# The next tile's preparation in a recurrent chain, issued behind the first half of the present tile's step

## The chip, the cores and the metric

The kernel runs on one core of a Trainium2 chip. Its time is the device time of one execution in microseconds (us). Engines are named as in the profile: PE (matrix multiplies; PEld its weight loads), DVE (the vector engine), ACT (the scalar engine), POOL (GpSimd) and SP (which issues the DMAs here). Each engine works through its own list of instructions in order; semaphores tell one engine that another, or a DMA, is done.

## The reference, cut to what matters

The model is two layers deep. In each layer 2304 tokens (256 of context, 2048 latent) are projected and pass three parallel groups of heads: a state-space scan, a gated delta rule (GDN) in both directions, and softmax attention. The part that the change touches is the GDN's scan over chunks of 64 tokens, for each of 4 heads and each direction:

```python
def step(S, inp):
    qd, kd, u_i, w_i, a_i, d_i = inp
    v_new = u_i - jnp.einsum('bhcd,bhde->bhce', w_i, S)
    o = jnp.einsum('bhcd,bhde->bhce', qd, S) + jnp.einsum('bhij,bhje->bhie', a_i, v_new)
    S = S * d_i[..., None, None] + jnp.einsum('bhcd,bhce->bhde', kd, v_new)
    return S, o
```

Every chunk needs the state S of the chunk before, so the 36 chunks of a layer are a chain. Attention needs nothing of it.

## The kernel before, in words

All values are 32-bit. In each layer the input projection comes first, then gating, the preparation of the GDN's chunk matrices (written to device memory), the state-space scan, then attention, and at the end the output projection. Attention is a list of 24 units of one head and 512 queries (`attention`, lines 623 to 675). For each unit, matmuls `pq` give scores of which DVE takes row maxima (`mx`, L533); then matmuls `pst` (L562, L563) give scores again, ACT takes the exponential (`pe`, L565), ACT and DVE split it into a high and a low part (`ph`, L570; `pl`, L571), and matmuls `po` (L556) multiply with the values. Three PSUM banks serve `pq` and `pst` while the chain runs.

`gdn_chain` (lines 1006 to 1182) runs beside attention, in the stretches of about 1340 to 1700 us (first layer) and 3300 to 3700 us (second). It handles both directions at once, one tile of 128 tokens of each direction per step, 18 steps to a layer, each of two halves (`for s in range(2)`), since a chunk is half a tile. Three functions make a step's work:

- `load(u)` (L1036) issues a tile's DMAs from SP into buffers that rotate among three tiles: `acv` (chunk matrices), `xu` and `xt` (parts of the triangular inverse), `kq` (keys and queries, called `kqc` in the profile) and `er` (decays). A buffer can be filled again only after the step three tiles earlier has read it.
- `prep(u)` (L1058) makes the loaded tile ready: DVE multiplies the keys by the decays (`kq[:, 0]`, L1060) and, where an output is wanted, masks `acv[:, :, 0]` (L1065), both in place; POOL makes `kdw` (L1062) and multiplies the queries (L1064); PE makes 16 small matmuls `pv` (L1071), ACT copies them to `vt` (L1075), PE makes 16 more from `vt` (L1080), and ACT copies these into `xu` (called `xf` in the profile; L1083).
- `step(u)` (L1086) does the two halves. In each, PE multiplies the state with the keys (L1104), DVE subtracts (`r`, L1108), PE multiplies by the inverse (L1118) and the queries (L1113), ACT copies `V` (L1123), PE makes the update and the output (L1127, L1129), and DVE adds the update to the decayed state `sd` (POOL, L1106), which gives the next state (`Sn`, called `Sc` in the profile; L1131).

`out(u)` (L1141) finishes an output tile. The loop at L1174 calls, for each u, `load(u + 2)`, `prep(u + 1)`, `step(u)` and `out` of a tile before. The order in which the calls are written isn't the order on the engines: the framework's scheduler places each instruction by a simulation of its own, and prefers what was written earlier among what it holds ready. Within `step` some matmuls are pinned by `behind` (L1002), which tells the scheduler that one instruction must stand after another of the same engine, with no semaphore.

Of the kernel before, what the change touches and what calls it, by code (L numbers as in the profile page):

```python
# [12 lines left out]
ALU = mybir.AluOpType  # L13
# [4 lines left out]
P = 128  # L18
# [66 lines left out]
def hybrid_kernel(ctx, tc, x, c, ctx_in, c_ctx, norm_w, w_mod, b_mod, w_in, conv_w, conv_b, ssd_A_log,  # L85
                  ssd_dt_bias, ssd_D, ssd_norm_w, gdn_A_log, gdn_dt_bias, gdn_norm_w, q_norm_w, k_norm_w,
                  w_out, cst_in, rope_in, eye_in, out):
    nc = tc.nc
# [23 lines left out]
    with tc.tile_pool(reuse_waits="tile", name="ini", bufs=1) as ini:  # L112
# [6 lines left out]
                                in1=sch[:, :, 0:2].bitcast(F32).rearrange("p k j -> p j k"), op=ALU.subtract)  # L119
# [124 lines left out]
    for l in range(DEPTH):  # L244
# [20 lines left out]
        with ExitStack() as ax:  # L265
# [118 lines left out]
            for g, (t0, ntl) in enumerate(GRP):  # L384
                for bi, (kind, c0, w, arg) in enumerate(blocks):
# [3 lines left out]
                    if kind == "n":  # L389
                        for u in range(ntl):  # L390
# [12 lines left out]
                            if arg < 2:  # L403
# [6 lines left out]
                                else:  # L410
# [7 lines left out]
                                    for o0, s0, n0 in ((0, 0, 50), (50, 62, 256)):  # L418
                                        nc.scalar.activation(out=zn[:, o0:o0 + n0], in_=ps[:, s0:s0 + n0], func=AF.Tanh, scale=0.5)
                                        nc.vector.scalar_tensor_tensor(out=zn[:, o0:o0 + n0], in0=zn[:, o0:o0 + n0], scalar=1.0,  # L420
                                                                       in1=ps[:, s0:s0 + n0], op0=ALU.add, op1=ALU.mult)
# [10 lines left out]
                    else:  # L432
                        for m in range(w // P):
# [12 lines left out]
                            for sb, (s0, sn) in enumerate(((0, 256), (256, 512)) if g == 0 else ((0, 384), (384, 384))):  # L446
# [6 lines left out]
                                for k in range(KD):  # L453
                                    for ww, hh in ((wh, hi), (wh, lo), (wl, hi)):
                                        nc.tensor.matmul(ps, ww[:, k, m * P:(m + 1) * P], hh[:, k, s0:s0 + sn],  # L455
                                                         start=(n == 0), stop=(n == 3 * KD - 1))
# [11 lines left out]
                            if kind == "t":  # L468
# [7 lines left out]
                                                               in1=acc[:, :n0], op0=ALU.mult, op1=ALU.add)  # L476
# [9 lines left out]
                                else:  # L486
                                    b0 = t0 * P - 1
# [3 lines left out]
        with ExitStack() as bx:  # L491
# [510 lines left out]
            def behind(mm, prev):  # L1002
                tc.add_manual_dep(mm.ins, prev.ins.name, mybir.DependencyInfo(
                    mybir.DependencyClass.NoSync, mybir.DependencyReason.DATA), reason="order")

            def gdn_chain(rq):
# [6 lines left out]
                with ExitStack() as gx:  # L1013
# [41 lines left out]
                            nc.sync.dma_start(er[dk[d]], eg_d[d:d + 1, :, u].to_broadcast([64, 4, P]))  # L1055
                        return u, xu, xt, kq, er, acv

                    def prep(u, xu, xt, kq, er, acv):  # L1058
                        want_o = u >= ot0
                        nc.vector.tensor_tensor(out=kq[:, 0], in0=kq[:, 0], in1=er, op=ALU.mult)  # L1060
                        kdw = gw.tile([P, 2, 4, 64], F32, name="kdw")
                        nc.gpsimd.tensor_tensor(out=kdw, in0=acv[:, :, 3], in1=kdc[:, u, :, :, None].to_broadcast([P, 2, 4, 64]), op=ALU.mult)  # L1062
                        if want_o:
                            nc.gpsimd.tensor_tensor(out=kq[:, 1], in0=kq[:, 1], in1=er, op=ALU.mult)  # L1064
                            nc.vector.tensor_tensor(out=acv[:, :, 0], in0=acv[:, :, 0], in1=msk[:, None, None, :].to_broadcast([P, 2, 4, 64]), op=ALU.mult)  # L1065
                        pv = slot("pv")
                        pvv = pv[:, 0:256].rearrange("p (c h n) -> p c h n", c=2, h=4)
                        for c in range(2):
                            for h in range(4):
                                for d in range(2):  # L1070
                                    nc.tensor.matmul(pvv[b1[d], c, h, :], acv[b0[d], 1 - c if d else c, 1, h, c1[d]], xt[b0[d], c, h, :],  # L1071
                                                     start=True, stop=True, tile_position=(b0[d].start, b1[d].start))
                        vt = gw.tile([P, 2, 4, 32], F32, name="vt")
                        for d in range(2):
                            nc.scalar.activation(out=vt[b1[d]], in_=pvv[b1[d]], func=AF.Copy, scale=-1.0)  # L1075
                        pzv = pv[:, 256:512].rearrange("p (c h n) -> p c h n", c=2, h=4)
                        for c in range(2):
                            for h in range(4):
                                for d in range(2):
                                    nc.tensor.matmul(pzv[b0[d], c, h, :], vt[b1[d], c, h, :], xu[b1[d], c, h, c1[d]],  # L1080
                                                     start=True, stop=True, tile_position=(b1[d].start, b0[d].start))
                        for d in range(2):
                            nc.scalar.copy(out=xu[b0[d], :, :, c1[d]], in_=pzv[b0[d]])  # L1083
                        return xu, kq, acv, kdw

                    def step(u, S, xu, kq, acv, kdw):  # L1086
                        tl = (u, rev(u))
                        want_o = u >= ot0
                        second = (u >= 1) if u < TC else (u >= TC + (NT - TC) // 2)
                        ox = op_ = None  # L1090
                        if want_o:
                            ox = gw.tile([P, 2, 4, 64], F32, name="ox")
                            if second:
                                op_ = gw.tile([P, 2, 256], F32, name="op_", bufs=1)
                                for d in range(2):
                                    by_chunk(d, o_d[tl[d]], op_)
                        for s in range(2):
                            cs = [slice(c * 64, c * 64 + 64) for c in (s, 1 - s)]
                            pab = slot("p")
                            pa = pab[:, 0:256].rearrange("p (h n) -> p h n", n=64)  # L1100
                            pb = pab[:, 256:512].rearrange("p (h n) -> p h n", n=64)
                            for h in range(4):
                                for d in range(2):
                                    nc.tensor.matmul(pa[tk[d], h, :], kq[dk[d], 0, h, cs[d]], S[dk[d], h, :], start=True, stop=True)  # L1104
                            sd = gw.tile([P, 4, 64], F32, name="sd")
                            nc.gpsimd.tensor_tensor(out=sd, in0=S, in1=dsc[:, u, s, :, None].to_broadcast([P, 4, 64]), op=ALU.mult)  # L1106
                            r = gw.tile([P, 4, 64], F32, name="r")
                            nc.vector.tensor_tensor(out=r, in0=acv[:, s, 2], in1=pa, op=ALU.subtract)  # L1108
                            po_ = want_o and slot("p")[:, 0:256].rearrange("p (h n) -> p h n", n=64)
                            prev = None  # L1110
                            for h in range(4):
                                for d in range(2 if want_o else 0):
                                    mm = nc.tensor.matmul(po_[tk[d], h, :], kq[dk[d], 1, h, cs[d]], S[dk[d], h, :], start=(h == 0), stop=False)  # L1113
                                    if prev is not None:
                                        behind(mm, prev)
                                    prev = mm
                                for d in range(2):
                                    mm = nc.tensor.matmul(pb[tk[d], h, :], xu[tk[d], (s, 1 - s)[d], h, :], r[tk[d], h, :], start=True, stop=True)  # L1118
                                    if prev is not None:
                                        behind(mm, prev)  # L1120
                                    prev = mm
                            V = gw.tile([P, 4, 64], F32, name="Vc")
                            nc.scalar.copy(out=V, in_=pb)  # L1123
                            pc = slot("p")[:, 0:256].rearrange("p (h n) -> p h n", n=64)
                            for h in range(4):
                                for d in range(2):
                                    nc.tensor.matmul(pc[dk[d], h, :], kdw[tk[d], s, h, :], V[tk[d], h, :], start=True, stop=True)  # L1127
                                for d in range(2 if want_o else 0):
                                    nc.tensor.matmul(po_[tk[d], h, :], acv[tk[d], s, 0, h, :], V[tk[d], h, :], start=False, stop=(h == 3))  # L1129
                            Sn = gw.tile([P, 4, 64], F32, name="Sc")  # L1130
                            nc.vector.tensor_tensor(out=Sn, in0=sd, in1=pc, op=ALU.add)  # L1131
                            if want_o:
                                nc.scalar.copy(out=ox[:, s], in_=po_)
                            S = Sn
                        if want_o and not second:
                            for d in range(2):
                                by_chunk(d, o_d[tl[d]], ox.rearrange("p c h n -> p c (h n)"), store=True)
                            ox = None
                        return S, None if ox is None else (ox, op_)

                    def out(u, ox, op_):  # L1141
                        tl = (u, rev(u))
# [31 lines left out]
                    for u in range(NT):  # L1174
                        if u + 2 < NT:
                            ahead.append(load(u + 2))
                        cur, nxt = nxt, prep(*ahead.pop(0)) if ahead else None
                        S, ox = step(u, S, *cur)
                        if pend is not None:
                            out(*pend)  # L1180
                        pend = (u, *ox) if ox is not None else None
# [129 lines left out]
```

## Time and profile before

| | |
|---|---|
| Runs of the kernel | 3998.72, 4003.42, 4008.57 us (median 4003.42) |
| Profiled execution | 3989.31 us |
| Its span | 3987.5 us |
| Mean granted clock of TensorE | 0.975 |
| PE busy | 3758.9 us, 94% of the span |
| DVE busy | 2704.5 us, 68% |
| ACT busy | 1799.1 us, 45% |
| POOL busy | 1347.3 us, 34% |

Busy shares are of the whole span. A stretch of it is read from tables by window, which give each engine's busy time between two instants, and the granted clock of TensorE there (1.00 is its higher level of 2.4 GHz, 0.50 its lower of 1.2 GHz). The idle time of an engine is put down to the instruction that came after it and to what that one waited for.

### The profile page before, as it was taken

How to read it: one execution, taken by the hardware profiler on the slowest of the kernel's cores; microseconds unless marked ns; L12 is line 12 of the kernel's file. 1: busy time of each engine (PE TensorE's matmuls, PEld its weight loads, DVE VectorE, ACT ScalarE, POOL GpSimd, SP SyncE). 2: the span in 40 equal slices, each digit the busy share in tenths (PEclk: the TensorE clock that was granted, in tenths of full speed). 3: DMA queues.
4: the chain of work that ended last, by engine and by line, in shares of the span. 5: the costliest groups of instructions: out<-in, count | busy, mean ns of one | idle time of the engine just before them, and what ended most of it. 6: DMA issues, size and time to landing. Idle time of an engine off the chain costs nothing. (4 is left out here: it accounts for less than half of the span.)

```text
span 3987.5 us, 70354 instructions
## 1 busy us (share of the span) xinstructions
PE 3758.9 (94%) x25750; PEld 2817.7 (71%) x25750; DVE 2704.5 (68%) x5372; ACT 1799.1 (45%) x3728; POOL 1347.3 (34%) x1762
## 2 busy tenths in 40 slices
PE   7999999988999898898999999999989999999989
PEld 5899999554466565565678999996544666656667
DVE  7556474789878566784547574755889876777733
ACT  5343342433466465574214443423333665566710
POOL 5112030376477322412213040302874662133010
PEclk8999999999999999998999999999999999999999
DMA  6343432354222654535744433332442226454244
GB/s 204 99 142 117 135 101 98 96 152 150 72 61 59 121 130 111 134 90 159 240 149 131 149 113 125 119 109 68 148 147 86 59 59 140 110 129 101 82 143 154
DMA packets 549798, 477.72 MB, mean 120 GB/s; under 512 B 133128, under 2 KB 487372, under 8 KB 549452
## 3 DMA queue, kind: packets, MB, share of 16 engines
q1 hardware_dynamic: 507596, 437.82, 37.6%
q10 hardware_dynamic: 41856, 35.40, 2.9%
q8 instruction: 203, 3.33, 0.3%
q14 instruction: 143, 1.17, 0.1%
HBM read 328.91 MB, written 144.18 MB: 119 GB/s over the span
## 5 line engine op out<-in xcount | busy, mean ns | idle before, releaser
L565 ACT ACTIVATE pe<-pst 128x512 f32<-128x512 f32 (+1 forms) x876 | 512.2, 594 | 619.7 <-PE pst L563 588.7
L533 DVE TENSOR_REDUCE mx<-pq 128x1 f32<-128x512 f32 (+1 forms) x972 | 589.5, 626 | 115.7 <-PE pq L531 112.0
L531 PE MATMUL pq<-khh,q 128*128 128x512 f32 (+1 forms) x972 | 456.6, 498 | 43.6 <-DVE mx L533 38.2
L556 PE MATMUL po<-pe,v 128*65 128x512 f32 x960 | 489.0, 598 | 1.8 <-ACT os__11676 L579 1.2
L562 PE MATMUL pst<-q,khh 128*128 128x512 f32 (+1 forms) x876 | 429.0, 490 | 25.5 <-DVE mx L533 23.2
L455 PE MATMUL ps<-lo,wh 128*128 128x384 f32 (+2 forms) x1296 | 441.2, 340 | 0.0
L455 PE MATMUL ps<-hi,wl 128*128 128x384 f32 (+2 forms) x1296 | 441.0, 340 | 0.0
L455 PE MATMUL ps<-hi,wh 128*128 128x384 f32 (+2 forms) x1296 | 440.9, 340 | 0.0
L401 PE MATMUL ps<-wh,hi 128*128 128x320 f32 (+1 forms) x1120 | 354.2, 318 | 1.3 <-DVE hi L365 1.2
L563 PE MATMUL pst<-qm,klo 65*128 65x512 f32 (+1 forms) x876 | 353.8, 405 | 0.0
L401 PE MATMUL ps<-wh,lo 128*128 128x320 f32 (+1 forms) x1120 | 350.0, 315 | 0.7 <-DVE lo L366 0.7
L401 PE MATMUL ps<-wl,hi 128*128 128x320 f32 (+1 forms) x1120 | 350.6, 314 | 0.0
L571 DVE TENSOR_TENSOR pl<-pe,ph 128x512 fp32r<-128x512 f32 x396 | 296.7, 755 | 72.3 <-ACT ph L570 38.2
L531 PEld LDWEIGHTS pq<-khh,q 128*128 128x128 f32 x972 | 184.8, 192 | 205.5 <-DVE mx L533 84.3
L376 DVE TENSOR_TENSOR wl<-wt,wh 128x1024 fp32r<-128x1024 f32 (+3 forms) x144 | 176.4, 1254 | 159.4 <-ACT wh L375 159.4
L570 ACT CAST ph<-pe 128x512 fp32r<-128x512 f32 x396 | 242.9, 620 | 61.0 <-DVE pl L571 21.9
L562 PEld LDWEIGHTS pst<-q,khh 128*128 128x128 f32 x876 | 168.4, 192 | 135.3 <-issue 53.9
L556 PE MATMUL po<-ph,vh 128*65 128x512 f32 x792 | 256.4, 405 | 1.3 <-ACT ph L570 0.7
L455 PEld LDWEIGHTS ps<-lo,wh 128*128 128x128 f32 x1296 | 244.0, 188 | 10.7 <-issue 0.4
L455 PEld LDWEIGHTS ps<-hi,wl 128*128 128x128 f32 x1296 | 243.4, 188 | 10.4
L455 PEld LDWEIGHTS ps<-hi,wh 128*128 128x128 f32 x1296 | 243.5, 188 | 10.3
L1238 PE MATMUL psd<-woh,mh 128*128 128x512 f32 x544 | 220.9, 406 | 18.1 <-ACT mh L1229 16.6
(588 smaller groups left out, 8094.2 us busy)
## 6 DMA issues: line engine op xcount, KB each, us to landing
wt<-in_w_in_dram SPq DMA_DIRECT2D x72, 512.0 KB
wmt<-in_w_mod_dram SPq DMA_DIRECT2D x48, 512.0 KB
pre_d<-pre SPq DMA_DIRECT2D x34, 512.0 KB
acv<-pre_d SPq DMA_DIRECT2D x34, 512.0 KB
kqc<-kt_d SPq DMA_DIRECT2D x68, 256.0 KB
acv<-pre_d SPq DMA_DIRECT2D x68, 256.0 KB
wt<-in_w_in_dram SPq DMA_DIRECT2D x24, 668.0 KB
wt<-in_w_in_dram SPq DMA_DIRECT2D x24, 640.0 KB
```

The lines of the kernel that those rows point to most:

```text
L376: nc.vector.tensor_tensor(out=wl[:, ks, :], in0=wt, in1=wh[:, ks, :].bitcast(F32), op=ALU.subtract)
L401: nc.tensor.matmul(ps, hh[:, k, a], ww[:, k, :], start=(n == 0), stop=(n == 3 * KD - 1))
L455: nc.tensor.matmul(ps, ww[:, k, m * P:(m + 1) * P], hh[:, k, s0:s0 + sn], start=(n == 0), stop=(n == 3 * KD - 1))
L531: nc.tensor.matmul(pq[:, :n], q2[:, u * P:(u + 1) * P], khh[:, kvh, k0t * P + a:k0t * P + a + n], start=True, stop=True)
L533: nc.vector.tensor_reduce(mx[:, i:i + 1], pq[:, :n], axis=AX.X, op=ALU.max)
L556: nc.tensor.matmul(po[0:65, :qn], v[:, kt, vs], p[:, :qn], start=(kt == k0t and j == 0), stop=(kt == k1t - 1 and j == len(ops) - 1))
L562: nc.tensor.matmul(pt[:, :qn], khh[:, kvh, ks], q2[:, :qn], start=True, stop=False)
L563: nc.tensor.matmul(pt[:, :qn], klo[:, kvh, ks], qm[:, :qn], start=False, stop=True)
L565: nc.scalar.activation(out=pe[:, :qn], in_=pt[:, :qn], func=AF.Exp, scale=0.125)
L570: nc.scalar.copy(out=ph, in_=pe)
L571: nc.vector.tensor_tensor(out=pl, in0=pe, in1=ph.bitcast(F32), op=ALU.subtract)
L1238: nc.tensor.matmul(ps, a, w[k][:, n * 512:n * 512 + 512], start=(k == 0 and i == 0), stop=(k == KD - 1 and i == 2))
```

## The change

`step` becomes a generator that stops once, after its first half, and hands over two instructions of that half: the state's addition on DVE and the last matmul on PE. `prep(u + 1)` is now written after that stop, that is between the halves of `step(u)`, and it pins three kinds of its instructions: the two products on DVE stand behind the state's addition of the first half, and the 16 first matmuls stand behind the last matmul of the first half. Its instructions on POOL and ACT, its second group of matmuls and the loads aren't pinned. No instruction is added or removed. The PSUM bank of `pv` is now taken between those of the two halves.

```diff
-                    def prep(u, xu, xt, kq, er, acv):
+                    def prep(u, xu, xt, kq, er, acv, after=None):
                         want_o = u >= ot0
-                        nc.vector.tensor_tensor(out=kq[:, 0], in0=kq[:, 0], in1=er, op=ALU.mult)
+                        ins = nc.vector.tensor_tensor(out=kq[:, 0], in0=kq[:, 0], in1=er, op=ALU.mult)
+                        if after:
+                            behind(ins, after[0])
...
                         if want_o:
                             nc.gpsimd.tensor_tensor(out=kq[:, 1], in0=kq[:, 1], in1=er, op=ALU.mult)
-                            nc.vector.tensor_tensor(out=acv[:, :, 0], in0=acv[:, :, 0], in1=msk[:, None, None, :].to_broadcast([P, 2, 4, 64]), op=ALU.mult)
+                            ins = nc.vector.tensor_tensor(out=acv[:, :, 0], in0=acv[:, :, 0], in1=msk[:, None, None, :].to_broadcast([P, 2, 4, 64]), op=ALU.mult)
+                            if after:
+                                behind(ins, after[0])
...
-                                    nc.tensor.matmul(pvv[b1[d], c, h, :], acv[b0[d], 1 - c if d else c, 1, h, c1[d]], xt[b0[d], c, h, :],
-                                                     start=True, stop=True, tile_position=(b0[d].start, b1[d].start))
+                                    mm = nc.tensor.matmul(pvv[b1[d], c, h, :], acv[b0[d], 1 - c if d else c, 1, h, c1[d]], xt[b0[d], c, h, :],
+                                                          start=True, stop=True, tile_position=(b0[d].start, b1[d].start))
+                                    if after:
+                                        behind(mm, after[1])
...
-                            nc.vector.tensor_tensor(out=Sn, in0=sd, in1=pc, op=ALU.add)
+                            ins = nc.vector.tensor_tensor(out=Sn, in0=sd, in1=pc, op=ALU.add)
                             if want_o:
                                 nc.scalar.copy(out=ox[:, s], in_=po_)
                             S = Sn
+                            if s == 0:
+                                yield ins, mm
...
-                        return S, None if ox is None else (ox, op_)
+                        yield S, None if ox is None else (ox, op_)
...
-                        cur, nxt = nxt, prep(*ahead.pop(0)) if ahead else None
-                        S, ox = step(u, S, *cur)
+                        st = step(u, S, *nxt)
+                        after = next(st)
+                        if ahead:
+                            nxt = prep(*ahead.pop(0), after)
+                        S, ox = next(st)
```

DVE before, in the first layer, from the end of step 1 (`Sc` is the new state, `kqc` the keys' product, `acv` the mask, `r` the subtraction, `mx`, `nm` and `pl` are attention's, `sso` and `ox` belong to `out`):

```order
L1131 TENSOR_TENSOR Sc<-sd,p 128x256
L1060 TENSOR_TENSOR kqc<-kqc,er 128x512
L571 TENSOR_TENSOR pl<-pe,ph 128x512
L533 TENSOR_REDUCE mx<-pq 128x1 x2
L571 TENSOR_TENSOR pl<-pe,ph 128x512
L1151 TENSOR_REDUCE sso<-sqo 128x8
L1108 TENSOR_TENSOR r<-acv,p 128x256
L1065 TENSOR_TENSOR acv<-acv,msk 128x2x256
```

This is the first half of step 2, and the two products are those of tile 4, the fifth `kqc` row of the list: the scheduler had placed the preparation nearly two steps ahead of its use. DVE now, from the end of the first half of step 2:

```order
L1137 TENSOR_TENSOR Sc<-sd,p 128x256
L1060 TENSOR_TENSOR kqc<-kqc,er 128x512
L1067 TENSOR_TENSOR acv<-acv,msk 128x2x256
L1164 TENSOR_TENSOR sso<-sso,rqr 128x8
L533 TENSOR_REDUCE mx<-pq 128x1 x2
L1167 TENSOR_TENSOR ox<-ox,zzg 128x512
L571 TENSOR_TENSOR pl<-pe,ph 128x512
L1114 TENSOR_TENSOR r<-acv,p 128x256
```

Here the two products are those of tile 3: a tile's products moved from the first half of the step two before its own to the second half of the step just before, three halves later, and they now stand next to each other behind the state. This holds from the second or third step on in both layers.

PE before, from the end of step 1, with the `pv` matmuls of tile 3 (`p<-Sc,kqc` is the state's first product):

```order
L1071 MATMUL pv<-xt__13036,acv 32x32 x16
L556 MATMUL po<-ph,vh_17038 65x512
L556 MATMUL po<-ph,vh_17039 65x512
L556 MATMUL po<-pl,vh_17038 65x512
L556 MATMUL po<-ph,vh_17038 65x512
L556 MATMUL po<-ph,vh_17039 65x512
L556 MATMUL po<-pl,vh_17038 65x512
L531 MATMUL pq<-khh,q_17353 128x512 x2
L562 MATMUL pst<-q_17052,khh 128x512
L563 MATMUL pst<-qm,klo 128x512
L1104 MATMUL p<-Sc,kqc 64x64 x8
L1080 MATMUL pv<-xf_12775,vt 32x32 x16
```

PE now, the `pv` matmuls of the same tile:

```order
L1075 MATMUL pv<-xt__13036,acv 32x32 x16
L531 MATMUL pq<-khh,q_17353 128x512
L562 MATMUL pst<-q_17052,khh 128x512
L563 MATMUL pst<-qm,klo 128x512
L531 MATMUL pq<-khh,q_17353 128x512
L556 MATMUL po<-pl,vh_17038 65x512
L556 MATMUL po<-ph,vh_17038 65x512
L556 MATMUL po<-ph,vh_17039 65x512
L556 MATMUL po<-pl,vh_17038 65x512
L1110 MATMUL p<-Sc,kqc 64x64 x8
L1119 MATMUL p<-Sc,kqc 64x64 x2
L1086 MATMUL pv<-xf_12775,vt 32x32 x16
```

On PE the group moved by one half, from the start of step 2 to its middle, and as before eight or nine of attention's matmuls and the state's product stand between it and the second group.

## Rows read from the trace of the kernel before

**Rows 1.** Page, part 1: busy time, share of the span, instructions

```profile
PE 3758.9 (94%) x25750; PEld 2817.7 (71%) x25750; DVE 2704.5 (68%) x5372; ACT 1799.1 (45%) x3728; POOL 1347.3 (34%) x1762
```

**Rows 2.** Table by window: the stretches of attention alone and of the chain

```profile
core 0: us, PE busy (x) PEld busy (x) DVE busy (x) ACT busy (x) POOL busy (x), PEclk, DMA share, GB/s
1200.00:1300.00 100.00, 99.32 (x450) 63.43 (x448) 77.81 (x170) 63.27 (x178) 71.42 (x77) 1.00 0.21 60
1340.00:1700.00 360.00, 317.70 (x4572) 210.17 (x4570) 245.61 (x455) 210.71 (x414) 107.56 (x95) 0.96 0.58 130
3300.00:3700.00 400.00, 367.28 (x4953) 241.99 (x4951) 280.37 (x527) 241.90 (x473) 113.84 (x106) 0.97 0.52 121
1700.00:1750.00 50.00, 49.92 (x514) 33.11 (x514) 44.47 (x91) 37.23 (x68) 13.32 (x12) 1.00 0.17 41
1700.00:1830.00 130.00, 126.26 (x835) 84.02 (x835) 100.93 (x179) 96.80 (x169) 13.32 (x12) 0.99 0.23 69
```

**Rows 3.** Groups by line, 1340 to 1700: busy, mean ns | idle before, releasers

```profile
L1060 DVE TENSOR_TENSOR kqc<-kqc,er 128x512 f32<-128x512 f32 x18 | 12.5, 693 | 47.3 <-DMA kqc<-kt_d 44.4 <-DMA er<-eg_d 2.2 <-DMA xt__13036<-xd_d 0.7
L1065 DVE TENSOR_TENSOR acv<-acv,msk 128x512 f32<-128x512 f32 x18 | 12.5, 692 | 33.5 <-DMA acv<-pre_d 13.6 <-issue 11.0 <-DMA er<-eg_d 4.7
```

**Rows 4.** The same groups, 3300 to 3700

```profile
L1060 DVE TENSOR_TENSOR kqc<-kqc,er 128x512 f32<-128x512 f32 x18 | 12.8, 712 | 36.2 <-DMA kqc<-kt_d 32.5 <-DMA er<-eg_d 3.5 <-issue 0.2
L1065 DVE TENSOR_TENSOR acv<-acv,msk 128x512 f32<-128x512 f32 x16 | 11.1, 692 | 27.7 <-DMA acv<-pre_d 18.2 <-DMA er<-eg_d 5.9 <-issue 2.3
```

**Rows 5.** Waits of PE, 1340 to 1700: total us, times, longest

```profile
PE po L556 <- DVE pl L571: 17.8, 13, 4.5
PE pq L531 <- DVE mx L533: 8.2, 6, 1.9
...
PE p L1104 <- DVE Sc L1131: 3.9, 2, 3.0
PE pv L1071 <- DMA xt__12791<-xd_d: 1.9, 1, 1.9
PE pv L1071 <- DMA xt__12808<-xd_d: 1.6, 1, 1.6
```

**Rows 6.** Timeline of SP, 1396 to 1400: start, us, instruction

```profile
1396.31 0.60 SPq L1054 DMA_DIRECT2D kqc<-kt_d  x1
...
1399.11 0.60 SPq L1054 DMA_DIRECT2D kqc<-kt_d  x1
```

**Rows 7.** Timeline of DVE, 1399 to 1405

```profile
1399.79 0.42 DVE L1131 TENSOR_TENSOR Sc<-sd,p 128x256 f32<-128x256 f32 x1
1403.09 0.69 DVE L1060 TENSOR_TENSOR kqc<-kqc,er 128x512 f32<-128x512 f32 x1 [2.88 <-DMA kqc<-kt_d]
1403.70 1.75 DVE L571 TENSOR_TENSOR pl<-pe,ph 128x512 fp32r<-128x512 f32 x1
```

**Rows 8.** Timeline of PE, 1399 to 1407

```profile
1399.62 0.69 PE L1071 MATMUL pv<-xt__13036,acv 32*32 32x32 f32 x32
...
1403.29 0.69 PE L1080 MATMUL pv<-xf,vt 32*32 32x32 f32 x32
...
1406.11 0.49 PE L531 MATMUL pq<-khh,q 128*128 128x512 f32 x1 [1.86 <-DVE mx L533]
```

**Rows 9.** Timeline of POOL, 1399 to 1405

```profile
1399.77 1.04 POOL L1062 TENSOR_TENSOR kdw<-acv,kdc 128x512 f32<-128x512 f32 x1 [0.91 <-PE p L1129]
...
1403.13 1.77 POOL L1064 TENSOR_TENSOR kqc<-kqc,er 128x512 f32<-128x512 f32 x1 [0.51 <-DMA kqc<-kt_d]
```

**Rows 10.** One line each: duration ns min/median/max, first and last start

```profile
L1106 POOL TENSOR_TENSOR sd<-Sc,dsc x72: 605/615/1069, 1330.7 to 3684.7; 128x256 f32<-128x256 f32 x72
L1075 ACT ACTIVATE vt<-pv x72: 373/377/382, 1346.3 to 3660.7; 32x256 f32<-32x256 f32 x72
L1083 ACT COPY xf<-pv x72: 363/364/368, 1349.4 to 3664.4; 32x256 f32<-32x256 f32 x72
```

**Rows 11.** Table by window, a stretch at the lower clock; columns as in rows 2

```profile
1384.30:1391.10 6.80, 4.22 (x12) 2.22 (x13) 5.15 (x9) 2.10 (x4) 2.74 (x2) 0.50 0.53 142
```

More of the change, by code (lines that the diff above doesn't have):

```diff
@@ L1126, in step @@
                                 for d in range(2):
-                                    nc.tensor.matmul(pc[dk[d], h, :], kdw[tk[d], s, h, :], V[tk[d], h, :], start=True, stop=True)
+                                    mm = nc.tensor.matmul(pc[dk[d], h, :], kdw[tk[d], s, h, :], V[tk[d], h, :], start=True, stop=True)
                                 for d in range(2 if want_o else 0):
-                                    nc.tensor.matmul(po_[tk[d], h, :], acv[tk[d], s, 0, h, :], V[tk[d], h, :], start=False, stop=(h == 3))
+                                    mm = nc.tensor.matmul(po_[tk[d], h, :], acv[tk[d], s, 0, h, :], V[tk[d], h, :], start=False, stop=(h == 3))
                             Sn = gw.tile([P, 4, 64], F32, name="Sc")
-                            nc.vector.tensor_tensor(out=Sn, in0=sd, in1=pc, op=ALU.add)
+                            ins = nc.vector.tensor_tensor(out=Sn, in0=sd, in1=pc, op=ALU.add)
                             if want_o:
```

## The prediction

> **What bounds the kernel now.** I read the busy shares first. PE is busy for 94% of the span, DVE for 68% [rows 1], so the sum of PE's idle time (some 229 us) is nearly all that an order of instructions can win. The table by window then says where it lies. In attention alone PE is busy for 99.32 of 100 us; in the chain's stretches it is busy for 317.70 of 360 and 367.28 of 400 us [rows 2]. That is 42.3 + 32.7 = 75.0 us of idle PE, and the change touches these stretches alone.
>
> Next, why PE idles there. The waits of PE name DVE: `po` waits for `pl`, `pq` for `mx`, both attention's own work [rows 5]. Yet DVE is busy for only 245.61 of 360 us, and where it is busier still, 44.47 of 50 us, PE keeps 49.92 [rows 2]. So DVE isn't short of time; it is held up. The groups by line show by what: before `kqc` it sat idle for 47.3 and 36.2 us, before `acv` for 33.5 and 27.7 us, nearly all until a DMA landed [rows 3, 4]. These 70 instructions held DVE for 144.7 us, 2.07 us each. One case in the timelines: the last load of `kqc` is issued at 1399.11 [rows 6], DVE finishes the state at 1400.21, stands before the product until 1403.09 [rows 7], and PE, which needs `mx` from behind it, idles for 1.86 us before 1406.11 [rows 8]. The reason is the order: the buffer is free only when the step three tiles earlier has ended, and DVE asks for the product of the new load at the start of the very next half.
>
> **The change part by part.** No instruction is added or removed; what moves are 36 + 34 products on DVE and 36 groups of `pv` on PE, less those of the first tile of each layer, which are not pinned.
>
> The products on DVE. A half takes about 360/36 = 10 us, and a tile's products now stand three halves later. The case above missed its load by 2.88 us, so each now has some 27 us to spare, and the 144.7 us of standing still go. What remains is their own time, 0.69 us each [rows 3], as before. What is late next: the block of both products behind the state, in front of `mx` and `pl`, 2 × 0.69 = 1.39 us. POOL's `sd` (0.615 us) is released by the same state [rows 10]. Rows show that such operations exclude each other: POOL's product takes 1.77 us when it starts with DVE's, against 1.04 us for `kdw` of the same shape [rows 9], and the `pl` behind takes 1.75 us [rows 7]. So the block is 1.39 us, or 1.39 + 0.62 = 2.0 us where `sd` gets between. Does PE feel it? Before, a block was 2.07 + 0.69 = 2.76 us and cost PE 75.0/70 = 1.07 us; attention's banks therefore cover about 1.7 us. A block of 2.0 us exceeds this by 0.3, over 34 steps 10 us; one of 1.39 us costs nothing. I take the 10. The upper bound is that PE feels the whole block: 34 × 1.39 = 47 us.
>
> The start of each chain. The first tile isn't pinned and its loads are as late as before: waits of PE for `xt` of 1.9 and 1.6 us and one of 3.0 us behind a late DVE [rows 5], 6.5 us. I leave them in.
>
> So PE's idle time falls from 75 to about 17 us: a gain of 58. Bounds: 75 - 0 = 75 and 75 - 47 - 6.5 = 21.
>
> The `pv` matmuls. They move by one half, cost the same 0.69 us [rows 8], and read loads that are by then older still; their PSUM bank is taken at another turn, but its last reader is then half a step back. Nothing, from either side; the rival below has the price if this is wrong. On POOL and SP the order stays nearly as it was: `kqc` on POOL still waits for fresh loads, but it holds up only `sd`, which is needed half a step later. In SP's list the loads of `xt` and `er` now stand behind a store of `ox` of the step just ended; they have more than a step until they are used. Nothing.
>
> The clock. Granted clock is 0.96 and 0.97 in the chain's stretches and 1.00 in attention alone [rows 2]; it drops after waits: PE idled 4.5 us [rows 5], and from 1384.3 to 1391.1 it ran at 0.50, the lower level [rows 11]. If PE's work bound all of that, the missing clock costs 0.04 × 360 + 0.03 × 400 = 26 us. If waits hide it, nothing: in the 6.8 us at the lower level PE was busy for 4.22 [rows 11]. Most of the waits that precede the drops go, but not those at the start, and part of the slow work is overlapped by idling that I have counted already. I take 14, about half, with 0 and 26 as ends.
>
> The Trainium skill bears on this one: "TensorE: Matmul & The Clock Gate", section "Terms", puts the cost at the time spent throttled, times one minus the granted share. By it the whole 26 us would be the price, and the sum would be 12 us better; the row of 1384.3, in which PE idles for over a third of the slow time, speaks for less.
>
> The sum: 58 + 14 = 72 us. Against the profiled execution, 3989.3 - 72 = 3917 us. That execution lies 14.1 us below the median of the runs shown, 4003.4; the runs of the changed kernel should stand the same way to their profile, so I predict 4003.4 - 72 = 3931 us. All of it counts at the end, since PE has attention left when the chain is done, at 126.26 of 130 us after it [rows 2], and then the output projection.
>
> **The rivals.**
>
> B, the new block becomes the wait. The two products stand without a gap, POOL's `sd` meets them every time, and PE feels all 1.39 us in each of 34 steps. For it: PE's `pq` and `po` did wait for `mx` and `pl` [rows 5], with three banks to bridge. Against it: the cover of 1.7 us above. Gain 21 us of idling plus some 5 of clock: 4003 - 26 = 3977 us. The Trainium skill, "SBUF — State Buffer", section "SBUF: two separate sides", says why these meet: VectorE with two SBUF inputs and GpSimd take one port pair in turn, each for a whole instruction. The trace agrees (1.77 against 1.04 us, [rows 9]). By that rule alone `sd` is in the way in every step, and B's condition is half met.
>
> C, it doesn't do what it says: another engine's order, POOL's products or SP's list with the store ahead of `xt` and `er`, delays the loads as much as the products moved, and DVE waits on. Against: 27 us of room. Time as before, 4003 us.
>
> D, slower. The second group of matmuls and `xu` now follow `pv` within one half, and are used in the next. If PE met each link without work between, `pv`, two `vt`, the second group and two `xf` would be 0.69 + 2 × 0.377 + 0.69 + 2 × 0.364 = 2.86 us [rows 8, 10] of waiting in 34 steps, 97 us, against the 75 won at best: 4003 + 22 = 4025 us. It decides above 75/34 = 2.2 us a step. Against it: eight of attention's matmuls and the state's product stand between the two groups, in the order now as before, and `xu` is wanted half a step, some 10 us, later.
>
> **How the numbers follow.** Forecast 0.76, B 0.13, C 0.06, D 0.05. The forecast's own range has the idle gain from 45 to 75 us and the clock's from 0 to 26: 4003 - 101 = 3902 to 4003 - 45 = 3958 us. The range reaches into B, to 3975, and down to 3900; what is left out is C, D and some of B, under 2 in 10. A measurement of this kernel can tell 0.3%, 12 us, from no change. Faster: the forecast and B, less B's nearer end, plus nothing of the others: 0.88. Within: C and that end: 0.08. Slower: D, less what of it stays within 12 us: 0.04.
>
> **What would show it.** In the profile after, the idle time of DVE before `kqc` and `acv` should fall from 144.7 us to under 15, at the chain's start alone; PE's idle time in the two stretches to about 17 us, its waits for `pl` and `mx` with it; the granted clock there to 0.98 or more. If DVE's idle time goes and PE's doesn't, it is B: the waits for `mx` right behind the products. If `kqc` and `acv` still wait for DMAs, it is C, and the SP list says which DMA stood ahead. If PE waits for `vt`, or `p<-r,xf` for `xf`, it is D. A gain under 45 us would make the cover of 1.7 us wrong, one over 101 us the claim that these stretches' idling is all there is to win.

## The result, and the profile after

The changed kernel takes 3906.87 us (median; 3904.35 to 3910.39), against 4003.25 us for the kernel before on the same chip (3998.72 to 4008.57): 96 us less by the medians; the ratio of the runs is 0.9763, with a 95% interval of 0.9748 to 0.9778. Predicted were 3931 us and a range of 3900 to 3975, so the result lies near the lower end of the range.

| | before | after |
|---|---|---|
| Median of the runs | 4003.25 us | 3906.87 us |
| Profiled execution, span | 3987.5 us | 3907.3 us |
| Mean granted clock | 0.975 | 0.978 |
| PE idle in the span | 228.6 us | 164.0 us |

The page's first part, as in [rows 1]:

```profile
PE 3743.3 (96%) x25750; PEld 2813.4 (72%) x25750; DVE 2714.8 (69%) x5372; ACT 1795.2 (46%) x3728; POOL 1349.3 (35%) x1762
```

DVE, ACT and POOL have the same work as before. To see where the 80.2 us of span went, the same work has to be compared, not the same microseconds. So here are, for each layer, the stretch from the chain's start to the last of attention's `po` matmuls; the table by window, first of the kernel before, then of the changed one (columns: stretch, its length, PE, PEld, DVE, ACT and POOL busy, clock, DMA share, GB/s).

```profile
1340.00:1827.50 487.50, 442.13 (x5399) 292.93 (x5397) 346.55 (x633) 306.92 (x581) 120.89 (x107) 0.96 0.49 114
3300.00:3802.80 502.80, 466.30 (x5376) 310.11 (x5375) 350.85 (x643) 312.76 (x592) 116.90 (x108) 0.97 0.46 112
```

```profile
1340.00:1789.60 449.60, 436.41 (x5419) 294.69 (x5416) 349.67 (x634) 307.67 (x585) 119.91 (x107) 0.98 0.54 127
3262.00:3722.90 460.90, 452.39 (x5391) 306.52 (x5390) 359.40 (x645) 312.61 (x595) 116.07 (x114) 1.00 0.50 122
```

The stretches became 37.9 and 41.9 us shorter, 79.8 in all: the whole difference of the spans lies here. PE's idle time in them fell from 45.4 + 36.5 = 81.9 to 13.2 + 8.5 = 21.7 us, a gain of 60.2; PE's busy time fell from 908.4 to 888.8 us for the same matmuls, a gain of 19.6, while the granted clock rose from 0.96 and 0.97 to 0.98 and 1.00.

The cause that the prediction named, DVE's idle time before the two products, answers to [rows 3, 4]. Groups by line of the changed kernel, 1340 to 1700 and then 3220 to 3700 us (times | busy, mean ns | idle before, releaser):

```profile
L1067 DVE TENSOR_TENSOR acv<-acv,msk 128x512 f32<-128x512 f32 x18 | 17.8, 986 | 3.4 <-issue 3.4
L1060 DVE TENSOR_TENSOR kqc<-kqc,er 128x512 f32<-128x512 f32 x18 | 13.2, 731 | 0.0
...
L1067 DVE TENSOR_TENSOR acv<-acv,msk 128x512 f32<-128x512 f32 x16 | 16.4, 1025 | 0.0
L1060 DVE TENSOR_TENSOR kqc<-kqc,er 128x512 f32<-128x512 f32 x18 | 13.5, 752 | 0.5 <-DMA er<-eg_d 0.4
```

That is 3.9 us instead of 144.7. The last load of one tile's keys and the product that needs it, timelines of SP and DVE:

```profile
1399.91 0.58 SPq L1054 DMA_DIRECT2D kqc<-kt_d  x1
...
1425.43 0.42 DVE L1137 TENSOR_TENSOR Sc<-sd,p 128x256 f32<-128x256 f32 x1
1425.77 0.68 DVE L1060 TENSOR_TENSOR kqc<-kqc,er 128x512 f32<-128x512 f32 x1
1426.37 1.10 DVE L1067 TENSOR_TENSOR acv<-acv,msk 128x512 f32<-128x512 f32 x1
```

From issue to product it was 3.98 us before, of which DVE stood still for 2.88 [rows 6, 7]; now it is 25.86 us, and DVE goes from the state into the product without a gap. POOL's `sd` of the same moment:

```profile
1418.69 0.61 POOL L1112 TENSOR_TENSOR sd<-Sc,dsc 128x256 f32<-128x256 f32 x1
1425.92 1.00 POOL L1112 TENSOR_TENSOR sd<-Sc,dsc 128x256 f32<-128x256 f32 x1 [2.69 <-DVE Sc L1137]
```

It takes 1.00 us here where the two products run and 0.61 where they don't, and the mask takes 1.10 instead of 0.69: they exclude each other, as the prediction had it from [rows 9]. This agrees with the Trainium skill, "SBUF — State Buffer", section "SBUF: two separate sides", by which VectorE with two SBUF inputs and GpSimd take a port pair in turn.

What PE still waits for, from the chain's start to the last `po` of the first layer, then of the second (total us, times, longest); it answers to [rows 5]:

```profile
PE po L556 <- DVE pl L571: 5.1, 4, 3.3
PE pv L1075 <- DMA xt__12791<-xd_d: 2.2, 1, 2.2
PE po L556 <- ACT os__17339 L579: 2.0, 1, 2.0
...
PE pq L531 <- DVE mx L533: 0.2, 1, 0.2
...
PE po L556 <- DVE pl L571: 4.9, 4, 3.1
...
PE pq L531 <- DVE mx L533: 0.6, 2, 0.4
```

Of the waits for `mx` right behind the products next to nothing is left. The longest wait for `pl`, 3.3 us, has a cause of its own, a DVE instruction of attention that stands before its load:

```profile
1572.20 0.68 DVE L533 TENSOR_REDUCE mx<-pq 128x1 f32<-128x512 f32 x1
1576.74 0.30 DVE L635 RECIPROCAL sm<-sm 128x24 f32<-128x24 f32 x1 [3.86 <-DMA sm<-sm_d]
1576.96 0.63 DVE L571 TENSOR_TENSOR pl<-pe,ph 128x512 fp32r<-128x512 f32 x1
```

### The profile page after: what moved, and what is told of

It is laid out like the page before. It is cut to its first block, busy times and chain, and to the rows that moved or that the text cites. A ratio compares the mean times of both kernels' runs of the same rounds, so it can differ in the third digit from the quotient of the medians.

```text
span 3907.3 us, 70399 instructions
## 1 busy us (share of the span) xinstructions
PE 3743.3 (96%) x25750; PEld 2813.4 (72%) x25750; DVE 2714.8 (69%) x5372; ACT 1795.2 (46%) x3728; POOL 1349.3 (35%) x1762
## 5 line engine op out<-in xcount | busy, mean ns | idle before, releaser
L570 ACT CAST ph<-pe 128x512 fp32r<-128x512 f32 x396 | 242.8, 620 | 29.9 <-PE po L556 13.2
```

Source lines behind the costliest of these rows:

```text
L570: nc.scalar.copy(out=ph, in_=pe)
```

## The experiments

Theory L (late loads): DVE, which works in order, no longer asks for a load that has just been issued; attention's work behind it no longer stands still, and PE with it. Rival P (place): the block behind the first half's state, or the middle of the step, is what lets attention flow. Rival P2: the `pv` matmuls or the turn of the PSUM banks bring a part. In every run, PE's idle time is given for the same work as above: from the chain's start to the last `po` of each layer, both layers added.

Of the pins, those on PE move nothing: built without them alone, the program has the same list of instructions on all five engines as the changed kernel. So no run was needed for them.

**No pins** (`e3_no_pins`).

```diff
-                        if after:
-                            behind(ins, after[0])
...
-                            if after:
-                                behind(ins, after[0])
...
-                                    if after:
-                                        behind(mm, after[1])
```

> The changed kernel without any of its pins; prep is still written between the halves. In the list of DVE a tile's two products then stand in the first half of the step before its own, apart from each other, two halves later than in the kernel before instead of three. Theory L (late loads: all that matters is that DVE no longer asks for a load that has not landed): a load missed by 2 to 3 us has 20 us of room, so DVE's idle time before the two products is under 15 us and the time is that of the changed kernel, 3900 to 3920 us. Rival P (place: it is the block behind the state, or the middle of the step, that lets attention flow): half of the gain at most, 3950 to 4000 us.

Measured: 4011.05 us, ratio 1.0027 (1.0013 to 1.0040). This is in neither range: L had 3900 to 3920 us, P 3950 to 4000. The condition of L, loads that have landed, was not met, as the profile shows. The groups by line of this kernel, 1340 to 1700 and 3220 to 3700 us:

```profile
L1060 DVE TENSOR_TENSOR kqc<-kqc,er 128x512 f32<-128x512 f32 x18 | 14.9, 827 | 38.2 <-DMA kqc<-kt_d 32.3 <-issue 3.4 <-DMA er<-eg_d 2.5
L1065 DVE TENSOR_TENSOR acv<-acv,msk 128x512 f32<-128x512 f32 x17 | 11.7, 690 | 17.2 <-DMA acv<-pre_d 9.3 <-issue 7.8
...
L1060 DVE TENSOR_TENSOR kqc<-kqc,er 128x512 f32<-128x512 f32 x18 | 14.2, 790 | 27.2 <-DMA kqc<-kt_d 24.5 <-DMA er<-eg_d 2.0 <-issue 0.7
L1065 DVE TENSOR_TENSOR acv<-acv,msk 128x512 f32<-128x512 f32 x16 | 11.0, 690 | 20.0 <-DMA acv<-pre_d 16.1 <-issue 3.9
```

DVE still stands still for 102.6 us, and a load issued at 1422.80 is asked for right away:

```profile
1422.80 0.60 SPq L1054 DMA_DIRECT2D kqc<-kt_d  x1
...
1426.82 0.69 DVE L1060 TENSOR_TENSOR kqc<-kqc,er 128x512 f32<-128x512 f32 x1 [2.51 <-DMA kqc<-kt_d]
```

I had counted the products in DVE's list wrongly by one tile: without pins the scheduler draws them forward to where they stood before, in the first half of the step two before their own. Writing `prep` later isn't what helps; the pin is. That the time is no better than before although 42 us of DVE's idle time are gone, I can't explain. The table by window of the two stretches (columns as above):

```profile
1340.00:1844.00 504.00, 456.27 (x5395) 303.33 (x5394) 353.31 (x633) 304.70 (x579) 120.18 (x107) 0.93 0.48 110
3316.50:3830.40 513.90, 476.73 (x5388) 317.82 (x5387) 358.86 (x644) 312.78 (x595) 116.85 (x113) 0.95 0.45 109
```

PE idles for 84.9 us, against 81.9 before, so its idle time didn't follow DVE's down; and its work takes 933.0 us instead of 908.4, at a lower granted clock. What PE loses isn't in proportion to the time that DVE stands still, and what lowered the clock stays open.

**The products alone** (`e4_products_alone`).

```diff
+                        then = ahead.pop(0) if ahead else None
+                        cur, nxt = nxt, prep(*then) if then else None
+                        st = step(u, S, *cur)
                         after = next(st)
-                        if ahead:
-                            nxt = prep(*ahead.pop(0), after)
+                        if then:
+                            products(*then, after)
```

(`products` holds the two pinned DVE products, which `prep` no longer has.)

> Only the two products on DVE are written and pinned behind the first half; the rest of prep (POOL, PE, ACT, the PSUM bank of pv) is written ahead of the step as in the kernel before. L: the whole gain, 3900 to 3920 us. Rival P2 (the pv matmuls or the turn of the PSUM banks bring a part of it): 3930 to 4000 us.

Measured: 3918.83 us, ratio 0.9796 (0.9778 to 0.9815), DVE idle 3.3 us before the products. At least the greater part of the gain is the two products'. All four runs (3916.70 to 3921.34 us) are longer than all of the changed kernel's, though the kernel before takes 4002.50 us on this chip, much as above, and PE idles for 30.4 us instead of 21.7: some 10 us may be due to the rest, as P2 has it, which this doesn't settle.

**Four buffers** (`e5_four_buffers`), on the kernel before.

```diff
-                        kq = gw.tile([P, 2, 4, P], F32, name="kqc", bufs=3)
-                        er = gw.tile([P, 4, P], F32, name="er", bufs=3)
-                        acv = gw.tile([P, 2, 4, 4, 64], F32, name="acv", bufs=3)
+                        kq = gw.tile([P, 2, 4, P], F32, name="kqc", bufs=4)
+                        er = gw.tile([P, 4, P], F32, name="er", bufs=4)
+                        acv = gw.tile([P, 2, 4, 4, 64], F32, name="acv", bufs=4)
...
-                        xu = xf[u % 3]
+                        xu = xf[u % 4]
```

> The kernel before with four buffers instead of three for kqc, er, acv and xf (xt keeps three): a load no longer waits for the step that ended a moment ago and is issued about a step earlier, while DVE's products stay in the first half of the step two before their own. L: DVE's idle time before the products falls from 145 us to under 25 us and most of the gain comes, 3905 to 3940 us. P: the order is the old one, so the time is too, 3990 to 4010 us.

Measured: 4009.12 us, ratio 1.0022 (1.0008 to 1.0036), no gain. The groups by line, 1340 to 1700 us:

```profile
L1065 DVE TENSOR_TENSOR acv<-acv,msk 128x512 f32<-128x512 f32 x18 | 13.3, 740 | 35.1 <-DMA acv<-pre_d 23.0 <-issue 5.3 <-DMA xt__12793<-xd_d 3.7
L1060 DVE TENSOR_TENSOR kqc<-kqc,er 128x512 f32<-128x512 f32 x18 | 12.4, 691 | 47.7 <-DMA kqc<-kt_d 40.7 <-DMA zzg<-zn_d 5.8 <-DMA er<-eg_d 1.2
```

With 37.3 and 25.7 us in the second layer DVE idles for 145.8 us, as before (144.7), and PE for 89.3. The number I forecast rested on the products staying where they were. They didn't: in DVE's list the scheduler put the product of tile k+3 into step k, one step further ahead, as it did with the load. The time is the one that P forecast, but with the loads as late as before it is also the one that L gives, so the run doesn't tell the two apart. It says something of its own: more buffers buy no room where a scheduler spends it at once.

**One half later** (`e6_one_half_later`).

```diff
+                        if u + 2 < NT:
+                            products(*ahead[1], after)
                         if ahead:
                             nxt = prep(*ahead.pop(0), after)
```

(`products` as above; those of the first two tiles are written ahead of the loop.)

> As the changed kernel, but the products of tile k+2, not k+1, are pinned behind the first half of step k: one half later than in the kernel before instead of three. L: a half is 10 us and the loads were late by 2 to 3 us (longest 4.6 us), so one half is enough: DVE idle before the products under 15 us, 3900 to 3920 us. Rival M (the loads, now crowded into a shorter chain, need more room): 30 to 70 us of that idle time stay, 3935 to 3975 us.

Measured: 3920.16 us, ratio 0.9796 (0.9773 to 0.9818). DVE idles before the products for 22.6 us (12.9 and 9.7 by layer), more than the 15 of L and less than the 30 of M; PE idles for 29.6 us, and most of the gain is there. The loads were late by a few us, and 10 us are almost enough.

**The changed kernel again, and the products at their old place** (`e7_changed_again`, `e10_same_place`).

```diff
                         ins = nc.vector.tensor_tensor(out=kq[:, 0], in0=kq[:, 0], in1=er, op=ALU.mult)
                         if after:
                             behind(ins, after[0])
...
                             if after:
-                                behind(ins, after[0])
+                                behind(ins, after[1])
...
+                        r0 = next(st)
+                        if then:
+                            products(*then, last_s and (last_s, r0))
```

(The first part is cut from `products`; the rest of `prep` is written ahead of the step, as in the kernel before. `last_s` is the state's addition at the end of the step before, `r0` the subtraction of the first half.)

> The changed kernel once more, on the chip of the next three, as their yardstick: 3900 to 3912 us.

> The two products at the places they had within a step in the kernel before (the keys' product at the start of the first half, the mask behind r, not in one block), but of tile k+1 instead of k+2, by pins; the rest of prep as in the kernel before. So the loads have one step (20 us) more and the place is the old one. L: the whole gain, 3900 to 3925 us, DVE idle before the products under 15 us. P (the block behind the first half's state is what lets attention flow): half of the gain at most, 3950 to 4003 us.

Measured: 3904.80 us for the changed kernel, ratio 0.9752 (0.9736 to 0.9769), and 3909.68 us for the old place, 0.9764 (0.9745 to 0.9784). The first product stands right behind the last state, the mask behind `r`, as in the order before, only for the next tile instead of the one after. The groups by line of the old place, 1340 to 1700 and 3220 to 3700 us:

```profile
L1059 DVE TENSOR_TENSOR kqc<-kqc,er 128x512 f32<-128x512 f32 x18 | 19.6, 1091 | 1.8 <-DMA er<-eg_d 1.8
L1063 DVE TENSOR_TENSOR acv<-acv,msk 128x512 f32<-128x512 f32 x18 | 16.7, 925 | 5.4 <-issue 5.4
...
L1059 DVE TENSOR_TENSOR kqc<-kqc,er 128x512 f32<-128x512 f32 x18 | 20.4, 1136 | 2.3 <-DMA er<-eg_d 2.3
L1063 DVE TENSOR_TENSOR acv<-acv,msk 128x512 f32<-128x512 f32 x16 | 14.5, 907 | 0.0
```

DVE's idle time before them is 9.5 us, PE idles for 26.1 us, and the two times can't be told apart: the gain is the whole one. P is refuted: neither the block nor the middle of the step is needed. This is what the first run of the series was meant to show.

**A longer block** (`e9_longer_block`).

```diff
+                        if after:
+                            behind(nc.vector.tensor_tensor(out=pad, in0=pad, in1=pad, op=ALU.mult), after[0])
```

> The changed kernel with a needless product of 128x1024 put between the two products in each step: DVE's block behind the state grows from 1.39 us by about 1.25 us, with no load in it. My estimate in the prediction was that attention's banks cover about 1.7 us of such a block and PE pays the rest: 34 times about 1 us, 25 to 50 us slower than the changed kernel. Rival: a block whose length the scheduler knew when it placed PE's work costs little, since other matmuls are put beside it: under 12 us slower; it was the surprise that cost, not DVE's time.

Measured: 3906.76 us, ratio 0.9756 (0.9737 to 0.9775): no cost that can be told from nothing. The block in its timeline:

```profile
1410.72 0.41 DVE L1141 TENSOR_TENSOR Sc<-sd,p 128x256 f32<-128x256 f32 x1
1411.05 0.68 DVE L1062 TENSOR_TENSOR kqc<-kqc,er 128x512 f32<-128x512 f32 x1
1411.65 1.21 DVE L1066 TENSOR_TENSOR pad<-pad 128x1024 f32<-128x1024 f32 x1
1412.79 0.68 DVE L1071 TENSOR_TENSOR acv<-acv,msk 128x512 f32<-128x512 f32 x1
```

From the start of the first product to the end of the mask these are 2.42 us, one of the shortest; over both layers the 34 blocks take 2.9 us on average, about as long as a late product held DVE before, 2.76 us. PE idles for 25.8 us, against 21.7; by my estimate, 34 times the 1.2 us above a cover of 1.7, it would have been some 40 us more. The cover is refuted, and with it rival B of the prediction. The scheduler knew this block's length when it placed the other engines' work; it didn't know of the late loads. That this is why the one costs and the other doesn't is my reading; the run shows only that it doesn't.

**The sums later** (`e8_sums_later`).

```diff
+                    yield
-                    nc.vector.reciprocal(sm[:, :w], sm[:, :w])
+                    ins = nc.vector.reciprocal(sm[:, :w], sm[:, :w])
+                    if seen:
+                        behind(ins, seen[-1])
```

(`seen` holds the newest row maximum `mx`; the second half of `inv` is called a unit of attention later.)

> The changed kernel with one more instruction moved past its load: the reciprocal of attention's sums (L635, on DVE), which stands still for 3.9 us in each layer beside the chain, is pinned about one unit of attention later. By L the same cure works again: PE's waits of 3.3 and 3.1 us for pl behind it go, with the drops of the clock after them (6.8 and 3.4 us at the lower level): 6 to 12 us faster than the changed kernel, 3895 to 3902 us. Rival: the wait is hidden or only moves to the next DMA: within 4 us of the changed kernel.

Measured: 3895.51 us, ratio 0.9738 (0.9721 to 0.9756), in its profile, which is the shortest of its runs, a span of 3884.9 us against 3901.9. DVE's wait before the reciprocal beside the chain is gone in both layers, here in the first:

```profile
L636 DVE RECIPROCAL sm<-sm 128x24 f32<-128x24 f32 x1 | 0.3, 293 | 0.0
```

The median is 9.3 us under the 3904.80 us of the changed kernel, as expected, but the intervals overlap: the wait's end is shown, the further gain is likely and not shown. Its median is the lowest here.

## Why the prediction was right

**What bounds the stretch.** As read: DVE's standing before the two products was the cause of PE's idling. It went from 144.7 to 3.9 us (under 15 forecast), and the experiments leave no other cause for most of the gain: every version in which the wait goes (3.3, 9.5, 22.6 us of it left) gains 80 us or more, and both in which it stays (102.6, 145.8) gain nothing. PE's idle time goes the same way: 18.4 to 30.4 us where the wait is gone, 81.9 to 89.3 where it stays. Open are how much of the wait costs how much, since 102.6 us cost as much as 144.7, and some 10 us between the products alone and the changed kernel.

**The idle time.** 58 us forecast, 60.2 measured, in stretches that reach further than the prediction's and so began with 81.9 us instead of 75.0. The sum of what remains was nearly right, 17 against 21.7 us, but not its parts, and that is partly luck. The block behind the state, for which I took 10 us, costs nothing that a run shows: the cover of 1.7 us, inferred from waits for late loads, was the weak step. The chain's start cost 2.2 us of PE's waits instead of 6.5. In their place came what I hadn't named: the reciprocal that waits for its load, with 3.3 and 3.1 us of PE. In the kernel before it came when its load had landed, with no idle time before it (1605.6 us); now DVE reaches it at 1572.88 us, before its load is issued at 1573.4. The other 13 us lie in waits of at most 2.0 us each.

**The clock.** 14 us forecast between 0 and 26, 19.6 measured as the fall of PE's busy time. The trace's record of the clock has the lower level for 61.4 us of the two stretches before and for 23.9 us after. The rule that the prediction weighed ("TensorE: Matmul & The Clock Gate", "Terms", of the Trainium skill) makes half of the difference the gain, 18.8 us by this estimate. The trace agrees, with 19.6. The longest part that stayed stands at the first chain's start, behind PE's wait for `xt` (columns as above):

```profile
1351.90:1362.20 10.30, 10.30 (x104) 6.94 (x100) 6.57 (x13) 4.90 (x10) 3.54 (x3) 0.50 1.14 193
```

So the gain is less than the whole price because 23.9 us at the lower level stayed, as the prediction said of the start, and not because waits hide slow work, its second reason: PE was busy for 58 of the 61.4 us before. The row that it took for this, with 4.22 of 6.80 us busy [rows 11], is the exception.

**The size of the whole.** 72 us forecast against 79.8 in the profiled executions and 96 between the medians of the runs. The last 16 are the step from profile to runs: I took it that both kernels' runs stand 14 us above their profile. The changed kernel's median lies 2 us below its profiled time of 3909.08 us, so this term was mis-sized: how far one execution stands from the others doesn't carry over to another kernel. It makes 16 of the 24 us by which the forecast lies too high; the other 8 are 2 of idle time and 6 of clock.

**The rivals.** B: refuted by the longer block. C: the change does what it says; but it is the pins on DVE that do it, and without them it would have been C. D: no wait of PE for `vt` or `xf` is among those left.

## What to carry to other kernels

When an in-order engine is idle for much of its time and yet late, look for the instruction that asks for a load just issued: its wait is paid by everything queued behind it, here by another part of the program. The cure here was to place the two instructions later: 10 us brought most of the gain, a step of about 20 us the whole. The scheduler drew them forward again when nothing pinned them, with four buffers a step further; a pin on that engine held them. That its simulation takes the loads to be faster than they are is inferred from this, not shown. And when such a wait goes, look for the next instruction that now comes before its load.

## What the runs showed of the hardware that was not expected

Two products that meet POOL's `sd` take longer in sum than alone, but the kernel's time doesn't show it: the mask's mean rose from 0.69 to 0.99 and 1.03 us, DVE's busy time in the two compared stretches from 697.4 to 709.1 us, while PE's idle time there fell to 21.7 us.
